# A decoder trunk's weight splits, ranked 40 instructions behind their place in the program

## The chip, the cores and the metric

The kernel runs on one core of a Trainium2 chip. The metric is the device time of one execution in microseconds (us); "before" has the median of three timed runs, and one further execution was profiled. The engines that matter here are PE (TensorE, matrix products), ACT (ScalarE), DVE (VectorE), POOL (GpSimd) and SP (SyncE, which issues every DMA of this kernel).

## The reference, cut to what matters

Input and output are 512 tokens of 1024 float32 features. Two residual layers and a last normalisation are computed:

```python
z = rms_norm(x, g) @ w_in                 # layer 0: 1024 -> 8208 columns
ya = forgetting_attention(qa, ka, va, log_f)   # 16 heads of 64
yb = dilated_attention(qb, kb, vb)             # 16 heads of 64
x = x + concat([ya * silu(ga), yb * silu(gb)]) @ w_out
z = rms_norm(x, g) @ w_in                 # layer 1: 1024 -> 6144 columns
y = head_group_norm(retention(rotate(q), rotate(k), v))   # 4 heads
x = x + (y * silu(g)) @ w_out
return rms_norm(x, final_norm)
```

All weights together are read once, in float32. The precision that the reference needs is kept by splitting each operand `a` into a high part (a rounded copy) and a low part (what the rounding left), and by adding three products: high times high, high times low, low times high.

## The kernel before

**Chunks of weights.** Every projection is cut into chunks of 128 x 1024 float32 (512 KB), which stand in one list, `plan`, in the order of their use. `load_next` (L163) issues the DMA of the next chunk into a tile `w_raw`. `split_next` (L170) takes the oldest loaded chunk and makes `w_h` and `w_l` of it: `split` (L140) lets ACT write the high part (L142) and DVE the low part, as raw minus high (L144, or L146 where a gain is multiplied in). It does so in two halves, or in as many pieces as the chunk has row blocks where the layer's norm gain is folded in (`kt0`). Then it calls `load_next`. `w_raw`, `w_h` and `w_l` have three buffers each, and a few chunks of the last stages have homes of their own.

**When a chunk is split.** A projection asks for a chunk with `weights()` (L201), which first splits another chunk if fewer than three are ready, so a split stands two chunks ahead of its use in the program. The projections of 512 columns (`proj_wide`, L284, used for v and the gate of layer 1) have their own such rule. Most chunks are used by 24 matmuls of 512 columns, three per `three()` (L210).

**Attention among projections.** In layer 0, eight groups of four heads follow each other. `interleave` (L351) alternates a step of attention with some matmuls of the next group's projections and of an output projection, by the matmul times that these add up. A step (`step`, L679) holds the score product and the softmax of one 128-row block (`softmax_block`: PE L538 and L539, DVE L542, ACT L544, DVE L545, POOL L546), the transposes of an earlier head's block and their split (`pth` and `ptl`, L553 and L142/L144), and its product with v (`ps_o`, L565 and L566). The evacuations of projections hang in between: `ka` and `kb` (L484, L485), `qa` (L142, L146, and five DMAs on SP), the gate (L527, L529). `finish_head` (L568) adds two halves (`y`, L580), multiplies by the gate on POOL (L582) and splits the result (`yh`, `yl`). Layer 1 does the same with `scores` (L815, with `a` at L825), `retain` (L828, with `bn`, `yn`) and `y_block` (L847), and with the rotation of q and k (`rt`, L778 to L787, the sums on POOL, then split into `qh` and `ql` or `kh` and `kl`).

**What sets the order.** The program is written as one sequence. A planner then walks it with durations of its own and deals the instructions out to the engines: each instruction has a rank, which counts up by one per instruction emitted, and whenever an engine is free in the planner's account, the ready instruction with the lowest rank goes next. What it finds is fixed as each engine's queue; on the chip an engine runs its queue strictly in that order, waiting on semaphores. POOL is exempt and runs in program order throughout; ACT and DVE are exempt in the first stage (L719 to L748), where the input's norms and transposes and the first two chunks' splits are.

The changed place is in `split_next`:

```python
if kt0 is not None:
    for k in range(shape[1]):
        split(h_[:, k], l_[:, k], src[:, k], scale=gain1[:, kt0 + k:kt0 + k + 1])
```

Of the kernel before, what the change touches and what calls it, by code (L numbers as in the profile page):

```python
# [60 lines left out]
def trunk(ctx: ExitStack, tc, x, even_norm, even_w_in, even_b_f, even_w_out,  # L61
# [14 lines left out]
    def r32(ap):  # L76
        return ap.bitcast(F32)
# [15 lines left out]
    gain1 = small[:, 8:8 + KT]  # L93
# [46 lines left out]
    def split(hi, lo, src, scale=1.0):  # L140

        act.activation(hi, src, AF.Copy, scale=scale)  # L142
        if isinstance(scale, float) and scale == 1.0:
            dve.tensor_tensor(lo, src, r32(hi), ALU.subtract)  # L144
        else:
            dve.scalar_tensor_tensor(lo, src, scale, r32(hi), ALU.mult, ALU.subtract)  # L146
# [16 lines left out]
    def load_next():  # L163
        if plan:
            src, *how = plan.pop(0)
            raw = wp.tile([P, src.shape[0] // P, src.shape[1]], F32, tag="raw", name="w_raw")
            dma(out=raw, in_=src.rearrange("(k p) c -> p k c", p=P))
            loaded.append((raw, *how))

    def split_next():  # L170
        if loaded:
            raw, de, tiles, kt0 = loaded.pop(0)
            shape = list(raw.shape)
            if tiles:
                h, l = tiles(shape)
            else:

                n, at = (16, 0) if de == "f" else (0, 8 if de == "v" else 0)
                h, l = (wp.tile([P, WCH], F32R, tag=tag, name=name)[:, at:at + 1024 + n * shape[1]].rearrange(
                    "p (k c) -> p k c", k=shape[1]) for tag, name in (("wh", "w_h"), ("wl", "w_l")))  # L180
            src, h_, l_ = raw, h, l
            if de == "f":
                fw = late["fw"].pop(0)
                split(h[:, :, 256:], l[:, :, 256:], fw)
                h_, l_ = h[:, :, 0:256], l[:, :, 0:256]
            elif de is True:
                src = raw.rearrange("p k (f two) -> p k two f", two=2)
                h_, l_ = (z.rearrange("p k (two f) -> p k two f", two=2) for z in (h, l))
            if kt0 is not None:
                for k in range(shape[1]):  # L190
                    split(h_[:, k], l_[:, k], src[:, k], scale=gain1[:, kt0 + k:kt0 + k + 1])
            else:
                n = shape[1] // 2
                for i in range(2):
                    sl = slice(i * n, (i + 1) * n)
                    split(h_[:, sl], l_[:, sl], src[:, sl])
            ready.append((h, l))
            count["split"] += 1
        load_next()

    def weights():  # L201

        if len(ready) < 3:
            split_next()
        count["used"] += 1
        return ready.pop(0)
# [77 lines left out]
    def proj_wide(w, c0, done):  # L284


        chunks = [(w[kc * 256:(kc + 1) * 256, c0:c0 + 512], False, fourth if kc == 3 else None, 2 * kc)
                  for kc in range(4)]

        def work():  # L290
            first, ws = count["used"], []
            for o in range(2):
                ps = [pp.tile([P, S], F32, tag="p", name="pw") for _ in range(2)]
                for kc in range(4):
                    if o == 0:
                        if count["split"] < first + 4:
                            split_next()
                        count["used"] += 1
                        ws.append(ready.pop(0))
                    h, l = ws[kc]  # L300
                    for i in range(2):
                        t = 2 * o + i
                        ts_ = slice(t * P, (t + 1) * P)
                        for k in range(2):
                            kt = 2 * kc + k
                            three(ps[i], xT[:, 0, kt, ts_], xT[:, 1, kt, ts_], h[:, k, :], l[:, k, :],
                                  kt == 0, kt == KT - 1)
                            if kt == KT - 1:
                                done(t, ps[i])
                            yield 3 * MM  # L310
                    if o and (kc < 3 or (loaded and loaded[0][2])):
                        split_next()
        return chunks, work(), 96 * MM
# [617 lines left out]
```

## Time and profile before

| | |
|---|---|
| median of 3 runs (lowest, highest) | 1008.86 us (1007.94, 1009.07) |
| profiled execution, its own time | 1007.19 us |
| its span on the core | 1005.4 us |
| granted TensorE clock, mean | 0.998 |

How to read the lines: the page gives for each engine its busy time, the share of the span and the number of instructions. A group of instructions reads: line, engine, operation, out<-in by the program's names, shapes, count, then busy time and mean nanoseconds of one, then the idle time of the engine before them and who ended it. A line of the timeline reads: start in us, duration in us, engine, line, operation, out<-in, shapes, count, and in brackets the idle time before it with who ended it. A line of PE's waits reads: who waited, who was waited for, us in total, how often, the longest. A view by tile gives durations as least, median and greatest nanoseconds with the first and last start. A stretch gives its length and each engine's busy time with the number of instructions. Matmul records overlap, and their ends are modelled.

### The profile page before, as it was taken

The page shows a single profiled execution, that of the slowest core. Times are in us where ns is not written, and L with a number is a line of the kernel's source. Part 1 is how long each engine was busy: PE and PEld are TensorE (multiplying, and loading weights), DVE is VectorE, ACT ScalarE, POOL GpSimd, SP SyncE. Part 2 cuts the span into 40 slices and gives each one's busy share as a digit, 9 for nine tenths or more (in the row PEclk, how much of TensorE's full clock was granted, in tenths as well). Part 3 has the DMA queues.
Part 4 walks back from the last instruction along what each step waited for, and adds up shares of the span by engine and source line. Part 5 has one row for each costly group of instructions (what it writes and reads, how often), then busy time and mean ns, then how long its engine had stood idle before and what let it go on. Part 6 is the DMA issues. An engine that isn't in the chain of part 4 may idle for free.

```text
span 1005.4 us, 14335 instructions
## 1 busy us (share of the span) xinstructions
PE 985.1 (98%) x5150; PEld 835.6 (83%) x5150; DVE 637.6 (63%) x1427; ACT 507.4 (50%) x1045; POOL 209.7 (21%) x315
## 2 busy tenths in 40 slices
PE   8999999999999999999999999999999999999997
PEld 6888898888888988988987789787888888888875
DVE  6458576586676676666668754658446834684475
ACT  6366465555645645655658664254434443444343
POOL 1011444445344441211213100201000200020001
PEclk9999999999999999999999999999999999999999
DMA  7554776544556694336433223222213322322112
GB/s 207 113 139 76 158 84 104 145 97 97 136 104 111 118 93 130 77 73 133 78 102 114 78 88 123 84 84 84 84 64 97 92 83 64 105 84 84 64 42 84
DMA packets 74296, 99.99 MB, mean 99 GB/s; under 512 B 6369, under 2 KB 49633, under 8 KB 74098
## 3 DMA queue, kind: packets, MB, share of 16 engines
q1 hardware_dynamic: 74226, 99.09, 42.4%
q8 instruction: 40, 0.66, 0.3%
q14 instruction: 30, 0.25, 0.1%
HBM read 84.36 MB, written 2.13 MB: 86 GB/s over the span
## 4 chain that ended last, share of the span: by engine, by line
PE 83%; DVE 6%; ACT 5%; DMA 2%; POOL 2%; issue 1%; SPq 0%; DVEq 0%; POOLq 0%; ACTq 0%
PE pf L211 10%; PE pf L212 10%; PE pf L213 10%; PE po L213 5%; PE po L211 5%; PE po L212 5%; PE pw L212 5%; PE pw L213 5%; PE pw L211 5%; PE pt L211 3%; PE pt L213 3%; PE pt L212 3%; PE ps_pt L553 3%; PE ps_o L566 2%; PE ps_s L539 2%; PE ps_o L565 2%
## 5 line engine op out<-in xcount | busy, mean ns | idle before, releaser
L211 PE MATMUL pf<-xT,w_h 128*128 128x512 f32 x512 | 202.1, 395 | 0.0
L213 PE MATMUL pf<-xT,w_l 128*128 128x512 f32 x512 | 200.3, 391 | 0.0
L212 PE MATMUL pf<-xT,w_h 128*128 128x512 f32 x512 | 200.2, 391 | 0.0
L144 DVE TENSOR_TENSOR w_l<-w_raw,w_h 128x512 fp32r<-128x512 f32 x190 | 136.8, 746 | 53.0 <-ACT w_h L142 41.4
L142 ACT ACTIVATE w_h<-w_raw 128x512 fp32r<-128x512 f32 x190 | 112.1, 624 | 92.6 <-PE pf L212 40.4
L546 POOL TENSOR_SCALAR pi<-pi,st 128x512 f32<-128x512 f32 (+3 forms) x128 | 74.8, 586 | 348.8 <-DVE st L545 311.8
L213 PEld LDWEIGHTS pf<-xT,w_l 128*128 128x128 f32 x512 | 96.1, 188 | 21.0
L211 PEld LDWEIGHTS pf<-xT,w_h 128*128 128x128 f32 x512 | 96.3, 188 | 17.7
L212 PEld LDWEIGHTS pf<-xT,w_h 128*128 128x128 f32 x512 | 96.3, 188 | 17.6
L142 ACT ACTIVATE w_h<-w_raw,small 128x256 fp32r<-128x256 f32 (+1 forms) x136 | 73.3, 596 | 71.7 <-PE pw L213 24.4
L146 DVE SCALAR_TENSOR_TENSOR w_l<-w_raw,small,w_h 128x256 fp32r<-128x256 f32 (+1 forms) x136 | 82.4, 641 | 35.9 <-ACT w_h L142 35.7
L142 ACT ACTIVATE pth<-ps_pt 128x512 fp32r<-128x512 f32 (+3 forms) x128 | 55.1, 431 | 85.3 <-PE ps_pt L553 78.9
L212 PE MATMUL pw<-w_l,xT 128*128 128x512 f32 x224 | 87.3, 390 | 1.2 <-DVE w_l L146 1.2
L211 PE MATMUL pw<-w_h,xT 128*128 128x512 f32 x224 | 88.1, 393 | 0.2 <-DVE rt L779 0.2
L213 PE MATMUL pw<-w_h,xT 128*128 128x512 f32 x224 | 87.3, 390 | 0.0
L544 ACT ACTIVATE pi<-pi,st 128x512 f32<-128x512 f32 (+3 forms) x128 | 71.4, 558 | 27.3 <-DVE st L542 26.6
L211 PE MATMUL pt<-w_h,xT 128*128 128x256 f32 x288 | 81.4, 283 | 0.3 <-ACT w_h L142 0.2
L212 PE MATMUL pt<-w_l,xT 128*128 128x256 f32 x288 | 80.8, 281 | 0.0
L213 PE MATMUL pt<-w_h,xT 128*128 128x256 f32 x288 | 80.6, 280 | 0.0
L333 DVE TENSOR_TENSOR xres<-po,xres 128x512 f32<-128x512 f32 x88 | 59.8, 684 | 27.7 <-PE po L213 27.6
L786 POOL TENSOR_TENSOR rt<-rt,rt 128x512 f32<-128x512 f32 x8 | 10.3, 1290 | 304.9 <-DVE rt L784 292.2
L144 DVE TENSOR_TENSOR ptl<-ps_pt,pth 128x512 fp32r<-128x512 f32 (+3 forms) x128 | 62.1, 487 | 14.8 <-ACT pth L142 12.6
(185 smaller groups left out, 2022.5 us busy)
## 6 DMA issues: line engine op xcount, KB each, us to landing
w_raw<-in_even_w_in_dram SPq DMA_DIRECT2D x64, 512.0 KB, 5.6
w_raw<-in_odd_w_in_dram SPq DMA_DIRECT2D x48, 512.0 KB, 3.7
w_raw<-in_even_w_out_dram SPq DMA_DIRECT2D x16, 512.0 KB, 4.1
w_raw<-in_odd_w_out_dram SPq DMA_DIRECT2D x16, 512.0 KB, 3.5
qb<-qa SPq DMA_DIRECT2D x32, 128.0 KB, 2.9
qb<-qa SPq DMA_DIRECT2D x16, 256.0 KB, 3.2
qa<-qa SPq DMA_DIRECT2D x32, 128.0 KB, 2.5
cs<-c_dram SPq DMA_DIRECT2D x16, 256.0 KB, 3.5
```

What stands on the lines that cost most here:

```text
L142: act.activation(hi, src, AF.Copy, scale=scale)
L144: dve.tensor_tensor(lo, src, r32(hi), ALU.subtract)
L146: dve.scalar_tensor_tensor(lo, src, scale, r32(hi), ALU.mult, ALU.subtract)
L211: pe.matmul(ps, lhsT=ah, rhs=bh, start=first, stop=False)
L212: pe.matmul(ps, lhsT=ah, rhs=bl, start=False, stop=False)
L213: pe.matmul(ps, lhsT=al, rhs=bh, start=False, stop=last)
L333: dve.tensor_tensor(xr, ps, xr, ALU.add)
L539: pe.matmul(ps[:, 0:n], lhsT=q[:, 1, qs], rhs=k[:, 0:n], start=False, stop=True)
L544: act.activation(pi[:, 0:n], pi[:, 0:n], AF.Exp, bias=st[:, 0:1], scale=-1.0, accum_out=st[:, 1:2])
L546: pool.tensor_scalar(pi[:, 0:n], pi[:, 0:n], st[:, 2:3], 1.0, ALU.mult, ALU.mult)
L553: pe.transpose(pt[:, (i - j) * P:(i - j + 1) * P], hs["p"][i][:, j * P:(j + 1) * P], ident)
L565: pe.matmul(po[:, j * P:S], lhsT=v, rhs=th[:, 0:n], start=(j == 0), stop=False)
```

## The change

The two loops that split a chunk are put under `tc.high_priority(offset=-40)`. Inside it, the rank counts on from 40 above its value; on leaving, it is set back to the value at entry. So each of a chunk's split instructions, on ACT and on DVE, ranks 40 behind its place, and all that follows, the chunk's `load_next` included, ranks as if the split instructions had not been counted. The extra piece that one projection takes from the forget gate's weights (`fw`, L184) stays outside. What is computed is the same.

```diff
-            if kt0 is not None:
-                for k in range(shape[1]):
-                    split(h_[:, k], l_[:, k], src[:, k], scale=gain1[:, kt0 + k:kt0 + k + 1])
-            else:
-                n = shape[1] // 2
-                for i in range(2):
-                    sl = slice(i * n, (i + 1) * n)
-                    split(h_[:, sl], l_[:, sl], src[:, sl])
+            with tc.high_priority(offset=-40):
+                if kt0 is not None:
+                    for k in range(shape[1]):
+                        split(h_[:, k], l_[:, k], src[:, k], scale=gain1[:, kt0 + k:kt0 + k + 1])
+                else:
+                    n = shape[1] // 2
+                    for i in range(2):
+                        sl = slice(i * n, (i + 1) * n)
+                        split(h_[:, sl], l_[:, sl], src[:, sl])
             ready.append((h, l))
```

## The prediction

> **What bounds the kernel now.** I read the page first, for the engines and the chain that ended last.
>
> ```profile
> span 1005.4 us, 14335 instructions
> PE 985.1 (98%) x5150; PEld 835.6 (83%) x5150; DVE 637.6 (63%) x1427; ACT 507.4 (50%) x1045; POOL 209.7 (21%) x315
> PE 83%; DVE 6%; ACT 5%; DMA 2%; POOL 2%; issue 1%; SPq 0%; DVEq 0%; POOLq 0%; ACTq 0%
> ```
>
> TensorE is busy for 985.1 of 1005.4 us. Reordering ACT and DVE takes no matmul away, so it can win no more than the 20.3 us in which PE stands still, and what lies ahead of the first matmul and behind the last stays. The second view says where those 20.3 us are: busy time by stretches of the span.
>
> ```profile
> core 0: us, PE busy (x) PEld busy (x) DVE busy (x) ACT busy (x) POOL busy (x), PEclk, DMA share, GB/s
> 0.00:25.00 25.00, 21.29 (x120) 17.08 (x121) 15.65 (x32) 15.20 (x29) 4.17 (x22) 1.00 0.78 208
> 130.00:200.00 70.00, 69.65 (x390) 60.39 (x390) 47.26 (x109) 38.93 (x85) 31.70 (x50) 1.00 0.65 113
> 480.00:550.00 70.00, 68.30 (x394) 58.67 (x394) 49.02 (x133) 48.14 (x111) 17.47 (x26) 1.00 0.36 91
> 640.00:700.00 60.00, 57.96 (x262) 47.74 (x263) 40.60 (x75) 24.60 (x42) 8.96 (x6) 1.00 0.29 88
> 800.00:900.00 100.00, 100.00 (x457) 83.11 (x456) 59.24 (x112) 39.41 (x67) 5.99 (x4) 1.00 0.28 85
> 970.00:1005.40 35.40, 27.26 (x126) 21.81 (x124) 20.92 (x54) 15.06 (x35) 5.54 (x4) 0.94 0.16 60
> ```
>
> The start lacks 3.7 us and the end 8.1. In the attention layer's steady state only 0.35 us are missing in 70; in the retention layer's steady state none in 100: there, a new order can lose and cannot win. The third view, PE's own waits, names what is left in between.
>
> ```profile
> PE ps_o L566 <- DVE ptl L144: 1.7, 5, 0.4
> PE pw L212 <- DVE w_l L146: 1.2, 1, 1.2
> PE ps_yt L852 <- ACT yn L844: 0.9, 1, 0.9
> PE pt L211 <- ACT w_h L142: 0.2, 1, 0.2
> ```
>
> PE waits for weights twice in the whole run: 1.2 us once on `w_l` and 0.2 once at the start. So the splits, which the change makes later, mostly come early enough. The two other rows are waits for results that DVE and ACT made beside splits, and these are what the change can win.
>
> **The change, part by part.** No instruction is added or removed, and the loads keep their numbers. What moves is the order in which the planner puts 326 pairs of full splits:
>
> ```profile
> L144 DVE TENSOR_TENSOR w_l<-w_raw,w_h 128x512 fp32r<-128x512 f32 x190 | 136.8, 746 | 53.0 <-ACT w_h L142 41.4
> L142 ACT ACTIVATE w_h<-w_raw 128x512 fp32r<-128x512 f32 x190 | 112.1, 624 | 92.6 <-PE pf L212 40.4
> L142 ACT ACTIVATE w_h<-w_raw,small 128x256 fp32r<-128x256 f32 (+1 forms) x136 | 73.3, 596 | 71.7 <-PE pw L213 24.4
> L146 DVE SCALAR_TENSOR_TENSOR w_l<-w_raw,small,w_h 128x256 fp32r<-128x256 f32 (+1 forms) x136 | 82.4, 641 | 35.9 <-ACT w_h L142 35.7
> ```
>
> They are 185 us of ACT's 507 and 219 of DVE's 638. A lower rank matters only where the planner has two ready instructions for one engine, and the other stands at most 40 behind the split. Where the split alone is ready, it goes as before.
>
> *How late can a split become?* By the page's row of engines, 5150 + 1427 + 1045 + 315 = 7937 instructions compute (weight loads belong to their matmuls). Forty of them hold 7.2 of DVE and 5.3 of ACT. At mean durations of 0.45 us (637.6/1427) and 0.49 (507.4/1045), that is 3.2 us on DVE and 2.6 on ACT: 6 us if all stood ready at once, which engines at 63% and 50% seldom see. *How much is there to spare?* Between 130 and 200 us, 20 half splits ran, so 10 chunks in 70 us, 7 us each:
>
> ```profile
> L142 ACT ACTIVATE w_h<-w_raw x20: 613/620/635, 133.4 to 196.9; 128x512 fp32r<-128x512 f32 x20
> L144 DVE TENSOR_TENSOR w_l<-w_raw,w_h x20: 672/693/1780, 134.1 to 198.1; 128x512 fp32r<-128x512 f32 x20
> ```
>
> With three buffers a split starts when the chunk three before it has been multiplied, and its own turn is two chunks later: 14 us, less the 1 to 5 us that a chunk's split takes. So 9 us are left and 6 at most are used; the delay costs nothing on PE there, because the multiplication of two earlier chunks covers it. The loads behind these splits start later by the same amount; the raw tiles have three buffers too, so a load has another two chunks, and I cost it at nothing. If that cover were gone, a late chunk would cost what the `pw` row above shows, 1.2 us.
>
> *What is won: the five waits at `ps_o`.* DVE just before the first of them, with PE's end of it:
>
> ```profile
> 170.84 0.76 DVE L144 TENSOR_TENSOR yl<-y,yh 128x512 fp32r<-128x512 f32 x1 [1.13 <-ACT yh L142]
> 171.52 0.68 DVE L144 TENSOR_TENSOR w_l<-w_raw,w_h 128x512 fp32r<-128x512 f32 x1
> 172.23 0.69 DVE L485 TENSOR_TENSOR kb<-pf,kb 64x512 fp32r<-64x512 f32 x1
> 172.95 0.56 DVE L542 CUSTOM_DVE_ANT_0 pi<-ps_s,bias 128x384 f32<-128x384 f32 x1
> 173.44 0.55 DVE L144 TENSOR_TENSOR ptl<-ps_pt,pth 128x384 fp32r<-128x384 f32 x1
> 173.27 0.42 PE L565 MATMUL ps_o<-pth,v 128*128 128x384 f32 x1
> 174.04 0.45 PE L566 MATMUL ps_o<-ptl,v 128*128 128x384 f32 x1 [0.35 <-DVE ptl L144]
> ```
>
> DVE runs without a break from `yl` to `ptl`, and the second half of a chunk's `w_l` is in that run with 0.68 us. Counted in the program, `pi` is emitted 9 instructions behind this split and `ptl` 17 behind: both get ahead of it, if the planner has `pi` ready. Then `ptl` ends 0.6 earlier, more than the 0.35 idle, and `w_l` comes behind it, 2 us later, with 9 to spare. The idle time understates the wait: 390 matmuls fit into those 70 us, 0.18 us each, while their records here are 0.4 long, so records overlap when PE runs freely, and up to some 0.15 more than the gap is lost. Bounds: nothing, and 5 times 0.5 = 2.5. I take 2.5.
>
> *What is won: the first retention block.*
>
> ```profile
> 678.87 1.78 DVE L146 SCALAR_TENSOR_TENSOR w_l<-w_raw,small,w_h 128x512 fp32r<-128x512 f32 x1
> 681.77 0.28 DVE L825 TENSOR_TENSOR a<-ps_a,dec 128x128 f32<-128x128 f32 x1
> 686.21 0.74 DVE L146 SCALAR_TENSOR_TENSOR w_l<-w_raw,small,w_h 128x512 fp32r<-128x512 f32 x1
> 688.32 0.69 DVE L778 TENSOR_TENSOR rt<-pf,rot 128x512 f32<-128x512 f32 x1
> 689.51 0.74 DVE L146 SCALAR_TENSOR_TENSOR w_l<-w_raw,small,w_h 128x512 fp32r<-128x512 f32 x1
> 691.18 0.75 DVE L841 SCALAR_TENSOR_TENSOR yn<-ps_r,mv,gate 128x512 f32<-128x512 f32 x1
> ```
>
> Three splits, 3.3 us together, lie in the stretch whose end PE awaits for 0.9 us. The one at 686.21 falls behind the rotation's `rt` (16 instructions later in the program), which only changes places inside the stretch. But the decay product `a`, which heads the retention block's own chain (scores, `a`, its split, the product with v, `bn`, `yn`), is emitted 11 instructions behind the split of 1.78 us at 678.87 and would go ahead of it. Bounds 0 and 0.9; I take 0.7, since 1.78 is more than the wait.
>
> *What it costs.* A new order on two queues makes new meetings: an instruction that the planner believed ready heads a queue while its input is late. The nearest rows are the waits themselves, 0.35 to 1.2 us each. Lower bound none, upper bound one in each of seven attention groups and four retention heads, 11 times 0.5 = 5.5. I take one or two, 0.6, because 5 waits of one kind in seven groups is what the order of before has.
>
> *The sum*: -2.5 - 0.7 + 0.6 = -2.6 us. The profiled execution took 1007.19 us (span 1005.4 and 1.8 around it) and becomes 1004.6. The median of the runs lies 1.67 above the profiled one, so 1008.86 - 2.6 = **1006.3**.
>
> **The rivals.** *Nothing decisive moves.* At 172.23 `kb`, emitted 4 ahead of that split, came behind it already: when the planner chose the split, `kb` was not ready in its account, and perhaps `pi` was not either. Then the five waits stay, and the sum is -0.7 + 0.6: 1008.8. For it: most splits start when PE frees their buffer, with the engine idle before them. Against it: DVE had stood idle for 1.13 us before `yl`, so the planner's account and the chip already part here, and `pi` is next in line.
>
> *Slower: late weights at the rotations.* The only real wait on weights has this queue:
>
> ```profile
> 641.71 1.47 DVE L146 SCALAR_TENSOR_TENSOR w_l<-w_raw,small,w_h 128x512 fp32r<-128x512 f32 x1
> 643.33 1.55 DVE L144 TENSOR_TENSOR ql<-rt,qh 128x512 fp32r<-128x512 f32 x1
> 645.03 0.69 DVE L144 TENSOR_TENSOR ql<-rt,qh 128x512 fp32r<-128x512 f32 x1 [0.15 <-ACT qh L142]
> 645.64 0.75 DVE L146 SCALAR_TENSOR_TENSOR w_l<-w_raw,small,w_h 128x512 fp32r<-128x512 f32 x1
> 795.20 1.47 DVE L146 SCALAR_TENSOR_TENSOR w_l<-w_raw,small,w_h 128x512 fp32r<-128x512 f32 x1
> 799.13 0.75 DVE L146 SCALAR_TENSOR_TENSOR w_l<-w_raw,small,w_h 128x512 fp32r<-128x512 f32 x1
> ```
>
> One half goes ahead of both `ql` and one behind, and PE waits 1.2 us for the second. If the first half also falls behind `ql`, PE waits for 0.75 more, and the same pattern at 795 us and in the other two heads turns into a wait of about 1.2 each: 0.75 + 3 x 1.2 = 4.4, **1013.2**. It decides from the point where the second half ends later than PE's last matmul of the chunk before; at 799.88 it did not, since PE waits for no other `pw` weights. Against it: `ql` is emitted ahead of the split already, so the demotion reorders nothing between these two.
>
> *Collision with POOL.* Splits with two SBUF inputs took 672 ns at best and 1780 at worst in the row above. The Trainium skill (SBUF — State Buffer, section Who interferes with whom) says that a VectorE instruction with two SBUF inputs and a GpSimd instruction that reads SBUF hold one port pair as a lock, the second waiting for the whole of the first; by that rule a split that is put off can land in a POOL operation that it now avoids. As a mechanism of this kernel, priced from rows: at the five waits, `w_l` would take 1.78 in place of 0.69, 1.1 more each, with the next softmax step behind it, 5 x 1.1 = 5.5 against the 2.5 won: **1011.9**. POOL there is quiet until its next `pi`, and a split that starts at about 173.4 is over by then:
>
> ```profile
> 174.56 0.59 POOL L546 TENSOR_SCALAR pi<-pi,st 128x384 f32<-128x384 f32 x1 [3.51 <-DVE st L545]
> ```
>
> The trace agrees with the lock (641.71 above: 1.47 us beside the rotation's POOL work, 0.75 without it), but at the place that counts it speaks against a hit.
>
> **How the numbers follow.** Forecast 0.45 (its own range 1004 to 1008), nothing decisive 0.33, late weights 0.14, collision 0.08. About 0.2%, 2 us, is what a measurement can tell from no change; faster means below 1006.8, slower above 1010.9. Of the forecast 0.32 is faster and 0.12 same, 0.01 slower; of the second 0.04, 0.27 and 0.02; late weights 0.01 same and 0.13 slower; collision 0.03 and 0.05. Together 0.36 faster, 0.43 same, 0.21 slower. Range: below, the gains at their bounds with no new wait and two or three more of PE's short waits gone, 1003; above, the collision at its price, 1012, which leaves out the late weights' full price.
>
> **What would show it.** Right: the row `ps_o L566 <- ptl` gone or down to one or two; `w_l` behind `ptl` at 172 us; the `ps_yt` wait shorter; steady retention still at 100.00 of 100. Wrong: PE waits on `w_h` or `w_l` beyond the two of now, `w_l` with a higher mean than 746 ns, or the same queue order at 172 us as before. The step I trust least is that the planner had `pi` ready.

## The result, and the profile after it

| | before | after |
|---|---|---|
| median of 19 runs (lowest, highest) | 1007.68 us (1006.68, 1009.61) | 1011.00 us (1008.35, 1013.73) |
| span of the profiled execution | 1005.4 us | 1008.8 us |
| ratio after to before, 95% interval | | 1.0027 (1.002 to 1.0035) |

The kernel became 0.27% slower, some 3 us. The forecast was 1006.3, 2.6 us less than the 1008.86 of its three runs; from the median of 19 runs, 1007.68, the same gain would have given 1005.1. The page of the changed kernel shows that no engine has more to do:

```profile
PE 983.2 (97%) x5150; PEld 835.3 (83%) x5150; DVE 634.1 (63%) x1427; ACT 507.4 (50%) x1045; POOL 209.2 (21%) x315
PE 87%; DVE 4%; DMA 4%; ACT 3%; issue 1%; POOL 1%; SPq 0%; POOLq 0%; ACTq 0%; DVEq 0%
```

In the chain that ended last, DMA's share is 4% where it was 2%. The stretches of the span, with the columns of the prediction's second view, say where:

```profile
62.00:130.00 68.00, 64.61 (x373) 55.81 (x372) 44.67 (x126) 37.48 (x87) 21.05 (x36) 1.00 0.56 104
130.00:200.00 70.00, 70.00 (x397) 60.93 (x396) 46.80 (x110) 39.21 (x86) 32.07 (x51) 1.00 0.66 114
270.00:340.00 70.00, 66.71 (x369) 57.44 (x367) 44.04 (x102) 36.24 (x80) 28.69 (x45) 1.00 0.57 108
800.00:900.00 100.00, 100.00 (x457) 83.11 (x456) 59.27 (x113) 39.53 (x68) 6.08 (x5) 1.00 0.28 85
```

Between 130 and 200 us PE is now busy without a gap, 70.00 of 70 where 69.65 stood: what the change was forecast to win there is won. But the stretch from 270 to 340 us lacks 3.29 us where it lacked 0.35, and the one from 62 to 130 lacks 3.39 where it lacked 1.08, by the row of before:

```profile
62.00:130.00 68.00, 66.92 (x391) 57.87 (x390) 45.80 (x127) 38.97 (x89) 21.70 (x36) 1.00 0.56 106
```

PE's waits in the changed kernel name the cause:

```profile
PE ps_s L539 <- DMA qa<-qa: 5.9, 2, 3.3
PE ps_pt L554 <- POOL pi L547: 2.0, 4, 0.8
PE pw L213 <- DVE w_l L146: 1.2, 1, 1.2
PE ps_yt L853 <- ACT yn L845: 1.0, 1, 1.0
```

The row `ps_o` on `ptl` is gone (lines from L189 on have moved down by one). The first row is new at this size. Before, it read:

```profile
PE ps_s L539 <- DMA qa<-qa: 0.3, 1, 0.3
```

The score product `ps_s` waits for the copies of `q` that SP sends from one half of the partitions to the other. The timeline has the larger of the two waits at 332.54:

```profile
332.54 0.68 PE L539 MATMUL ps_s<-ka,qa 128*128 128x512 f32 x2 [3.29 <-DMA qa<-qa]
```

**Why are the copies late?** DVE's timeline of the changed kernel, some 20 us earlier in the same group:

```profile
312.74 0.76 DVE L144 TENSOR_TENSOR yl<-y,yh 128x512 fp32r<-128x512 f32 x1 [1.13 <-ACT yh L142]
313.42 0.55 DVE L543 CUSTOM_DVE_ANT_0 pi<-ps_s,bias 128x384 f32<-128x384 f32 x1
...
314.73 0.56 DVE L144 TENSOR_TENSOR ptl<-ps_pt,pth 128x384 fp32r<-128x384 f32 x1
...
315.28 0.67 DVE L144 TENSOR_TENSOR w_l<-w_raw,w_h 128x512 fp32r<-128x512 f32 x1
```

This is the swap that the prediction wanted: `w_l` behind `pi` and `ptl`. But this `w_l` is also the last reader of a raw tile, and SP's next load waits for it. SP's issues before the change (start, duration, line, destination and source):

```profile
312.96 0.37 SPq L167 DMA_DIRECT2D w_raw<-in_even_w_in_dram  x1
318.39 0.37 SPq L167 DMA_DIRECT2D w_raw<-in_even_w_out_dram  x1
320.53 0.47 SPq L497 DMA_DIRECT2D qb<-qa  x1
...
325.03 0.53 SPq L498 DMA_DIRECT2D qa<-qa  x1
```

And after it:

```profile
316.01 0.37 SPq L167 DMA_DIRECT2D w_raw<-in_even_w_in_dram  x1
319.17 0.37 SPq L167 DMA_DIRECT2D w_raw<-in_even_w_out_dram  x1
321.10 0.47 SPq L498 DMA_DIRECT2D qb<-qa  x1
...
330.28 0.46 SPq L499 DMA_DIRECT2D qa<-qa  x1
```

The first load leaves 3.1 us later, 1.2 of which is what the whole kernel is behind at this point (`yl` starts at 312.74 in place of 311.57). The second load and the copies, which have other releasers, leave only 0.8 and 0.6 us later. So two loads of 512 KB, which stood 5.4 us apart, now stand 3.2 us apart, and the copies are issued 5.1 us behind the first instead of 7.6. The DMA issues of this stretch (KB each, median us from issue to landing), before:

```profile
w_raw<-in_even_w_in_dram SPq DMA_DIRECT2D x3, 512.0 KB, 7.9
w_raw<-in_even_w_out_dram SPq DMA_DIRECT2D x2, 512.0 KB, 4.5
qb<-qa SPq DMA_DIRECT2D x4, 128.0 KB, 2.7
```

and after:

```profile
w_raw<-in_even_w_in_dram SPq DMA_DIRECT2D x3, 512.0 KB, 8.6
w_raw<-in_even_w_out_dram SPq DMA_DIRECT2D x2, 512.0 KB, 7.0
qb<-qa SPq DMA_DIRECT2D x4, 128.0 KB, 7.2
```

The median copy of 128 KB takes 7.2 us where it took 2.7. The row of `w_out` mixes two loads: the one at 319.17 alone takes 9.6 us, where it took 4.1 before. The transfers stand in line: the first load, issued at 316.01, lands 9.6 us later, at 325.6, the second at 328.8, and the first copy, issued at 321.10, at 329.1. From 320 to 324 us the busy share of the 16 DMA engines is 0.97. The pieces `qa<-qa` overwrite what the `qb<-qa` copies read, so SP issues them only when those have landed, and it waits for that 13.9 us in place of 7.5 (the `qb<-qa` rows of SP's waits, first before, then after):

```profile
SPq L498 <- DMA qb<-qa: 7.5, 9, 1.2
```

```profile
SPq L499 <- DMA qb<-qa: 13.9, 10, 4.7
```

The Trainium skill (DMA: Bandwidth & Descriptors, section Queues, rings and completion order) says that each DMA engine takes the descriptors of one ring in order, so that a transfer issued later starts behind the earlier ones there. The copies' 7.2 us agree.

**Why only in two places?** A load is late in six groups. Five have the swap. In the first, the second half of chunk 14 fell behind another `pi` and ran beside POOL's product from 100.28 to 101.58 us (it took 1.41 us at 100.71, and 0.69 before), so its load left at 102.19 in place of 100.91. PE waits for the copies in two of the six, the first and the fourth. In the group at 172 to 200 us of the changed kernel the loads themselves are quicker:

```profile
w_raw<-in_even_w_in_dram SPq DMA_DIRECT2D x2, 512.0 KB, 4.9
```

One by one, in the order of the groups, these six loads took 8.3, 4.8, 6.0, 8.3, 5.1 and 5.2 us before the change. The two long ones are those of the two groups that lose: a late load of 6 us or less leaves the copies enough time, a late load of 8 does not. Why loads of the same size and row length take 4.8 us in one group and 8.3 in another is not explained by these runs; the same two were the long ones in every kernel here that kept these loads ahead of the copies.

### The profile page after: what moved, and what is told of

Read it like the earlier page. It is cut to its first block, busy times and chain, and to the rows that moved or that the text cites. A ratio compares the mean times of both kernels' runs of the same rounds, so it can differ in the third digit from the quotient of the medians.

```text
span 1008.8 us, 14346 instructions
## 1 busy us (share of the span) xinstructions
PE 983.2 (97%) x5150; PEld 835.3 (83%) x5150; DVE 634.1 (63%) x1427; ACT 507.4 (50%) x1045; POOL 209.2 (21%) x315
## 4 chain that ended last, share of the span: by engine, by line
PE 87%; DVE 4%; DMA 4%; ACT 3%; issue 1%; POOL 1%; SPq 0%; POOLq 0%; ACTq 0%; DVEq 0%
PE pf L212 10%; PE pf L213 10%; PE pf L214 10%; PE po L214 5%; PE po L212 5%; PE po L213 5%; PE pw L213 5%; PE pw L214 5%; PE pw L212 5%; PE ps_pt L554 3%; PE pt L212 3%; PE pt L214 3%; PE pt L213 3%; PE ps_o L567 2%; PE ps_o L566 2%; PE ps_s L540 2%
## 5 line engine op out<-in xcount | busy, mean ns | idle before, releaser
L144 DVE TENSOR_TENSOR w_l<-w_raw,w_h 128x512 fp32r<-128x512 f32 x190 | 133.9, 726 | 52.1 <-ACT w_h L142 40.3
```

## The experiments

The theory: the swapped half split delays a raw load, the load meets the copies of `q` on the DMA engines, and PE waits for these. The times below are medians with the ratio to the kernel before, run on the same chip (its median was 1008.97 in the first four, 1008.58 in the next four and 1008.27 in the last three).

**The six splits alone, and all but the six.** Chunk 14, which is in the first group, and the five chunks whose `w_l` fell behind `ptl`.

```diff
-            with tc.high_priority(offset=-40):
+            with (tc.high_priority(offset=-40) if count["split"] in (14, 24, 34, 44, 54, 64) else ExitStack()):
```

> Only six splits are demoted by 40: chunk number 14 in the list and, in each attention group from the second on, the one chunk whose second half of w_l fell behind ptl in the changed kernel (24, 34, 44, 54, 64). Theory (the swapped half split frees its raw tile about 3 us later, SP issues the next two loads later, and the five q copies that stand behind these loads land later than PE needs them): the five ps_o waits go (-2.5 us) and PE's wait on qa<-qa comes (about +5.5 us), so the time is that of the changed kernel, 1010 to 1011.5 us, and the profile has the row ps_s on DMA qa<-qa with 4 to 7 us and none for ps_o on ptl. Rival A (the loss comes from the other 157 demoted chunks, and the swap is a pure gain): 1005.2 us, no wait on qa<-qa.

Measured: 1011.28 us, ratio 1.0018 (1.0007 to 1.0028). PE's waits have the `qa<-qa` row and none for `ptl`:

```profile
PE ps_s L539 <- DMA qa<-qa: 4.6, 2, 2.3
```

The complement has `not in` in the same line.

> The other way round: every chunk is demoted by 40 but these six. Theory: the time is that of the kernel before within 1 us, 1007 to 1008.7 us; the ps_o waits are there (1.5 to 2 us), the wait on qa<-qa is 0.5 us at most. Rival A (the other demotions cost it): 1010.5 us or more, up to 1013.5 with the gain at ps_o gone too.

Measured: 1008.89 us, ratio 1.0001 (0.9991 to 1.0012). Its waits:

```profile
PE ps_pt L554 <- POOL pi L547: 2.3, 4, 0.9
PE ps_o L567 <- DVE ptl L144: 1.9, 5, 0.6
PE ps_s L539 <- DMA qa<-qa: 1.5, 1, 1.5
```

So the six splits alone give the change's effect, as far as the intervals can tell, and Rival A falls: the others, demoted, leave the time where it was. One thing missed: a wait of 1.5 us on `qa<-qa` in the first group, where 0.5 at most was expected. Part of the first group's wait can come without the swap, and why it did in this execution was not settled.

**The loads late, the compute order of before.** The kernel before, with a dependency of the six loads on the most recent `ptl`.

```diff
+            ld = dma(out=raw, in_=src.rearrange("(k p) c -> p k c", p=P))
+            if count["split"] - 1 in (15, 25, 35, 45, 55, 65):
+                tc.add_manual_dep(ld.ins, late["ptl"].ins.name, ...)
```

> The order of before on every compute engine; only six loads, those issued after the six splits, wait in addition for the most recent ptl, so SP issues them about 3 us later, as in the changed kernel. Theory: the wait on qa<-qa appears by itself (3 to 6 us in all) and the ps_o waits stay, so the kernel is slower than before and as slow as the changed one or slower: 1010.5 to 1013.5 us. Rival B (the q copies are late because of DVE's or ACT's new order, not because of the loads): 1007 to 1008.7 us, no wait on qa<-qa beyond 0.5 us.

Measured: 1021.81 us, ratio 1.0122 (1.0102 to 1.0143): the right sign, but 8 us more than expected. Its wait on the copies, and two stretches behind the longest part of it:

```profile
PE ps_s L541 <- DMA qa<-qa: 9.3, 3, 6.3
```

```profile
124.00:128.00 4.00, 2.87 (x7) 2.46 (x8) 0.32 (x1) 1.15 (x2) 0.00 (x0) 0.52 0.86 225
128.00:132.00 4.00, 4.00 (x15) 3.35 (x14) 2.92 (x11) 2.12 (x7) 2.21 (x4) 0.63 0.35 87
```

The `ps_o` waits on `ptl` stay (1.7 us), as they must, and the `qa<-qa` wait comes by itself: late loads alone are enough, and Rival B falls. The cleanest place is the fourth group, where every engine's order is that of before:

```profile
341.26 0.68 PE L541 MATMUL ps_s<-ka,qa 128*128 128x512 f32 x2 [2.55 <-DMA qa<-qa]
```

The size was missed on two counts. In the first group the load left at 108.25 in place of 100.91 us, 7 later and not 3, and PE waited 6.3; there the planner also dealt some instructions of PE, DVE and ACT out in another order, so that this part of the wait is not the load's alone. And after that wait the granted clock was 0.52 and 0.63 in two stretches of 4 us, which adds an estimated 3 us to the 6.3: 0.48 of 2.87 and 0.37 of 4.00 busy microseconds.

**The six splits 40 ahead.**

```diff
-            with tc.high_priority(offset=-40):
+            with (tc.high_priority(offset=40) if count["split"] in (14, 24, 34, 44, 54, 64) else ExitStack()):
```

> The same six splits are ranked 40 ahead of their place in place of 40 behind. Theory: the half split that stood between yl and ptl goes ahead of yl, so ptl comes some 0.7 us earlier and the raw tile is free earlier, not later: the ps_o waits shrink or go (-1.5 to -2.5 us), no wait on qa<-qa beyond 0.5 us, 1005 to 1006.5 us, less than both kernels. Rival C (the planner already puts the split as early as it believes it ready, so that a better rank moves nothing): the time and the ps_o waits of before, 1007 to 1008.7 us.

Measured: 1005.28 us, ratio 0.9961 (0.9946 to 0.9976). A second time, in another set of runs:

> The six promoted splits once more, to have the gain twice: ratio 0.995 to 0.9975; if the first measurement was luck of the loads, 0.998 to 1.001.

Measured: 1005.86 us, ratio 0.9975 (0.9964 to 0.9987). And without chunk 14, `(24, 34, 44, 54, 64)`:

> Five of the six splits ranked 40 ahead, without chunk 14 in the first group, where no ps_o wait stood: the order of PE, POOL and SP is that of before. Theory: the whole gain comes from the five: ratio 0.995 to 0.9975. If the first group was a part of it: 0.9975 to 0.999.

Measured: 1005.12 us, ratio 0.9969 (0.9957 to 0.998). In this last kernel, DVE at the place of the first of the five waits, and the stretch in which the changed kernel lost most:

```profile
169.37 1.78 DVE L144 TENSOR_TENSOR w_l<-w_raw,w_h 128x512 fp32r<-128x512 f32 x1
171.30 0.69 DVE L144 TENSOR_TENSOR yl<-y,yh 128x512 fp32r<-128x512 f32 x1 [0.15 <-ACT yh L142]
...
173.22 0.55 DVE L144 TENSOR_TENSOR ptl<-ps_pt,pth 128x384 fp32r<-128x384 f32 x1
```

```profile
270.00:340.00 70.00, 70.00 (x396) 60.96 (x396) 48.84 (x110) 39.08 (x86) 32.60 (x50) 1.00 0.61 114
```

The half split now stands ahead of `yl`, where DVE had been idle for 1.13 us, so none of it lies between `yl` and `ptl`, and the raw tile is not freed late. The stretch is full, and no wait on `qa<-qa` is left among those of PE: the same five waits are won without the price. Rival C falls. This version beats both kernels, by 0.3% the one before and, by the two ratios, 0.6% the changed one.

**The copies ahead of the load.** The changed kernel, with the six loads emitted behind the copies and dependent on the last `qa` piece.

```diff
+            if count["split"] - 1 in (15, 25, 35, 45, 55, 65):
+                late["load"] = [0, raw, src]
+            else:
+                dma(out=raw, in_=src.rearrange("(k p) c -> p k c", p=P))
...
+                        ld = dma(out=raw, in_=src.rearrange("(k p) c -> p k c", p=P))
+                        tc.add_manual_dep(ld.ins, low.ins.name, ...)
```

> The changed kernel, but in each of the six places the load that the late half split releases is emitted behind the ten q copies (two heads' pairs, five each) and depends on the last qa piece that DVE writes, so that the copies go ahead of it on SP's queue and on the DMA engines. Theory (the loads ahead of the copies are what makes PE wait): the wait on qa<-qa goes (0.5 us at most), the gain at ps_o stays, so the kernel is 2 to 3.5 us faster than the kernel before; the load is some 10 us later and has about 9 us of spare ahead of its own split, so a wait of PE on w_h or w_l of up to 1 us per group, 5 in all, is what could eat it. Rival D (the copies are slow by themselves, whatever stands ahead of them): the wait on qa<-qa stays at 3 to 6 us and the kernel is 1.5 to 3.5 us slower than before.

Measured: 1019.93 us, ratio 1.0116 (1.0097 to 1.0136). No wait on `qa<-qa` is left among those of PE, which speaks against Rival D; but the load went to 333.58 us, and DVE stood idle for 4.74 us before the next chunk's split at 343.55. A load that late is no longer covered: PE waits for `y`, 7.2 us where it waited 1.1 before, and for `pi` 5.3 where it waited 0.6. The planner also dealt the instructions out anew here, so the 11 us are not the price of one cause. With the six splits promoted as well, the result was the same:

> The six splits are ranked 40 ahead, and the six loads are emitted behind the q copies. Theory: with the splits ahead, only 0.35 us of wait on qa<-qa was left in the profile, so the reordered loads can bring 0.4 us at most: ratio 0.995 to 0.997, the same as the six promoted splits alone. If the later loads make PE wait for weights: ratio 0.997 to 1.002.

Measured: 1020.26 us, ratio 1.0117 (1.0099 to 1.0136), outside both expectations, with `ps_o` on `y` at 6.5 us.

**Shorter loads at the same place.** The changed kernel with the six loads from a contiguous block; these chunks' products are those of other weights.

```diff
+            n = count["split"] - 1
+            if n in (15, 25, 35, 45, 55, 65):
+                src_ = even_w_out[0][128 * (n // 10):128 * (n // 10) + 128, :].rearrange("p (k c) -> p k c", k=4)
+            dma(out=raw, in_=src_ if n in (15, 25, 35, 45, 55, 65) else src.rearrange("(k p) c -> p k c", p=P))
```

> The changed kernel, but the six loads read a contiguous block of w_out (rows of 4 KB) in place of their own 256 columns of w_in (rows of 1 KB); what is computed from these six chunks is therefore not the reference's product, while sizes, order and count of all work stay. Theory, if it is the time that the load takes on the DMA engines that pushes the copies back: the six loads land in 3 to 5 us in place of 8 to 10, the copies behind them land 3 to 5 us earlier, PE's wait on qa<-qa falls below 1 us and the kernel is 1.5 to 3 us faster than before. Rival E (the copies wait because SP issues them late, not because the DMA engines are busy): no change against the changed kernel, 1.5 to 3.5 us slower than before.

Measured: 1005.32 us, ratio 0.9968 (0.9955 to 0.9982). The DMA issues from 305 to 345 us, where the row of `w_out` has the replaced load among its three, and the stretch around them:

```profile
w_raw<-in_even_w_out_dram SPq DMA_DIRECT2D x3, 512.0 KB, 4.0
...
qb<-qa SPq DMA_DIRECT2D x4, 128.0 KB, 2.5
```

```profile
270.00:340.00 70.00, 70.00 (x396) 60.95 (x395) 46.68 (x109) 39.22 (x86) 31.47 (x50) 1.00 0.58 113
```

The order of before with the same short loads is the control:

> The control to the run with short loads: the kernel before with the same six loads from the contiguous block of w_out (again these six chunks' products are not the reference's). Theory: in the order of before the loads leave the copies in time but for 0.4 us, so short loads bring 0.5 us at most and the ps_o waits (2.5 us) stay: ratio 0.999 to 1.0005, about 3 us behind the changed kernel with the same loads. Rival F (short loads help any order by some 3 us for a reason of their own): ratio 0.996 to 0.998.

Measured: 1008.08 us, ratio 0.9997 (0.9989 to 1.0006), with `ps_o` on `ptl` at 1.7 us as ever. Short loads bring nothing to the order of before and turn the changed kernel's loss into a gain of 3 us. SP issues the loads and the copies in the same order as in the changed kernel, so Rivals E and F fall: it is the time that the late load spends on the DMA engines. Row length and source were changed together here; which of the two makes the load short was not separated.

**All splits 40 ahead.**

```diff
-            with tc.high_priority(offset=-40):
+            with tc.high_priority(offset=40):
```

> All chunks' splits are ranked 40 ahead of their place in place of 40 behind. Theory: the gain at ps_o is the one that six promoted splits gave (ratio 0.996), and the other 157 chunks have 9 us of spare either way, so their promotion brings nothing of itself: ratio 0.995 to 0.998. If evacuations and softmax pieces that PE waits for fall behind promoted splits, new waits of 0.4 to 1.2 us each appear: ratio 0.998 to 1.005. Rival: splits were late in many places, and the wait pw on w_l (1.2 us) and the waits near 513 to 570 us shrink too: ratio below 0.994.

Measured: 1008.05 us, ratio 0.9995 (0.9985 to 1.0005). The second branch of the expectation: only two waits of `ps_o` on `ptl` are left in the profile (1.2 us), but `y` (2.4 us where 1.1 stood before) and `qa<-qa` (1.8) take the gain back.

## Why the prediction was wrong

*What bounds the kernel* was read rightly: PE does, and the steady retention stretch stayed at 100.00 of 100.

*The five waits at `ps_o`, 2.5 us*, were right, place and size. The step trusted least, that the planner had `pi` ready, held; the windows went to 70.00 of 70. Where nothing was lost to the copies, the kernel gained 3.1 us (the five promoted splits) and 3.3 (the changed order with short loads), which the intervals do not tell from 2.5.

*The first retention block, 0.7 us*, was wrong: the wait is 1.0 where it was 0.9. The pair of splits still stands ahead of `kl` and `a`, in the changed kernel at

```profile
680.77 3.17 DVE L146 SCALAR_TENSOR_TENSOR w_l<-w_raw,small,w_h 128x512 fp32r<-128x512 f32 x2
683.86 1.28 DVE L144 TENSOR_TENSOR kl<-rt,kh 128x512 fp32r<-128x512 f32 x2
685.07 0.28 DVE L826 TENSOR_TENSOR a<-ps_a,dec 128x128 f32<-128x128 f32 x1
```

The step took a place within 40 ranks as enough; the row of `ps_o` was argued with a look at what was ready, this one was not. Why the planner did not put `a` first was not looked into. The reading was also incomplete: before the change five half splits start between 678.87 and 691.18 us, not three (the two others at 684.94 and 686.96), and `kl` stands between the first and `a`.

*New waits on the compute queues, 0.6 us*: there are such, `ps_pt` on `pi` went from 0.6 to 2.0, and others shrank; the run with all but the six, which has them (2.3), is as fast as before.

*The step that failed* is the sentence on the loads: that they "start later by the same amount", that "a load has another two chunks", and "I cost it at nothing". The first half was right: 3.1 us later, 1.9 of them against the rest of the group. The cover was also right for the load's own reader: PE waits for no `w_h` or `w_l` in the attention groups, and `pw` on `w_l` is 1.2 as before. (PE's waits on `w_h` at the start of the kernel are 1.3 us in two places, beyond the 0.2 of before. They do not follow the order: the run with short loads and the order of before has 2.2 there, the one with the six splits alone none.) But the cover was worked out for the load's reader alone, and not for what stands behind the load on SP's queue and on the DMA engines. The copies of `q` stand there, and the row `ps_s` on `qa<-qa`, 0.3 us, in the trace of before said that in one group they had no spare at all. That term is 5.9 - 0.3 = +5.6 us. In place of -2.5 - 0.7 + 0.6 the sum is then -2.5 + 0 + 5.6 = +3.1, with the compute queues' new and lost waits at nothing, beside 3.4 measured in the spans.

The 5.6 is that of one execution. Over the 19 runs the changed kernel took 1008.35 to 1009.43 us in the five whose mean granted clock was 0.998, and 1012.06 to 1013.73 in the four at 0.994; the profiled one took 1011.0 at 0.999. The others were not traced; presumably some of them lost less to waits and others had a lower clock on top. That the sum also meets the difference of the medians, 3.3, is then in part luck.

*The rivals* were all wrong as well. The order did change at the places named; weights at the rotations were not late; and at the five waits there was no collision with POOL (`w_l` at 315.28 took 0.67 us); the one in the first group, above, was not the place that the prediction had priced, and what it cost was the load's delay. A slower outcome had been given a fifth, for two reasons neither of which was the one. That 1011.0 still lies between the bounds 1003 and 1012 is luck: the upper one was the price of the POOL collision.

## What to carry to other kernels

A compute instruction that frees a buffer is, in effect, also the issue of the DMA that fills it: when it moves, follow that DMA to everything that is queued behind it, small copies above all, and not only to its own reader. A load's spare is the smaller of its reader's and of what it leaves to the transfers behind it. Where two instructions compete, see first whether the engine has idle time ahead of both: here the same half split, put ahead instead of behind, won the five waits at no price that these runs show.

## What the runs showed of the hardware

*A clock that falls after a wait.* Behind the 6.3 us wait above the granted clock was 0.52; in the run of the six splits alone it fell already behind a wait of 2.3 us, while the changed kernel kept 1.00 behind 3.29. Two stretches of the run of the six splits alone, with the wait in the first:

```profile
114.00:118.00 4.00, 1.71 (x6) 1.10 (x6) 0.00 (x0) 0.00 (x0) 0.00 (x0) 0.83 0.58 132
118.00:122.00 4.00, 4.00 (x16) 3.37 (x15) 1.91 (x7) 1.91 (x5) 0.59 (x1) 0.74 0.77 237
```

The Trainium skill (TensorE: Matmul & The Clock Gate, Part 1: The HAM clock gate (the "warmup" mystery)) gives half the clock after an idle window of about 3.4 us that runs freely. The long wait agrees; a fall after 2.3 us of waiting is earlier than that figure. In such executions a wait of PE costs more than its length.

*DMA engines that are full at 92 GB/s.* While the load of 1 KB rows runs, just ahead of the copies, the kernel before has, from 316 to 320 us, a DMA share of 0.95 at 92 GB/s, where its first 25 us had 0.78 at 208. GB/s alone would have shown room there; the share shows hardly any.
